# A hybrid decoder trunk: stream, embeddings and output transposed by the host, layer 0 projected before its norm

## The chip, the core and the metric

The kernel runs on one core of a Trainium2 chip. The metric is the device time of one launch in microseconds (us); what the host does before and after the launch is not in it. Most runs of one kernel agree within 0.3%.

## The reference

A sequence of 2048 tokens of width 1024 in float32 passes two layers. Layer 0 is half retention, half stick-breaking attention (4 heads of 128 each), layer 1 is an RWKV-7 recurrence (16 heads of 64). Each layer is followed by a gated embedding p, and the stream ends in an RMS norm.

```python
def rmsnorm(x, gain):
    y = xf * lax.rsqrt(jnp.mean(xf * xf, axis=-1, keepdims=True) + RMS_EPS)
    return y * gain
for i in range(2):
    hn = rmsnorm(h, norm_gain[i])
    if i % 2 == 0:   # z = hn @ w_in, split in q, k, v, gate of both groups
        h = h + even_mixer(hn, even_w_in, even_w_out, ret_gn_gain)
    else:
        h = h + rwkv7_mixer(hn, ...)
    gate = sigmoid(h @ ple_gate[i])
    h = h + gate * (p[i] @ ple_proj[i])
return rmsnorm(h, final_gain)
```

The factor 1/rms of a token is one number per row of hn, so `(x * gain / rms) @ w` equals `(x * gain) @ w` with each row scaled by 1/rms afterwards.

## The kernel before

The tokens go through in two halves of 1024 (`w` = 0, 1), in blocks of 512 (`TB`) or tiles of 128. Operands of the large projections are exact splits of float32 into two parts, hi and lo (`split`, L215 and L216), and each product is three matmuls (`mm3`, L246 to L248). `proj_T` gives results with a channel on a partition, `proj_N` with a token on a partition.

The order of the work: half 0 of layer 0 (`l0_norm`, `retention`, `stick`, `tail`), half 0 of layer 1's projections (`l1_proj`), half 1 of layer 0 (`l0_norm_next`, `retention`, `stick`), then layer 1's recurrence of half 0 merged with half 1's tail (`tail_lean`), `l1_proj` of half 1, the recurrence of half 1 merged with a further `tail_lean`, and a last `tail` over 512 tokens with the rest of the final norm beside it. A generator per piece says in what order instructions are written; a planner then places them on each engine by its own costs. Each engine and each DMA queue (SP's, ScalarE's, POOL's) works through its list in order.

What the change touches:

- `load_vectors` (L177) gathers nine vectors by DMA, and TensorE transposes them.
- `l0_norm` (L323): x comes in rows (a token on a partition). ScalarE sums squares (L342), VectorE forms 1/rms (`rsqrt`), two matmul groups spread it over partitions (L348), TensorE transposes x (L377), one copy goes to DRAM as the residual `xT` (L380), VectorE multiplies by gain and 1/rms (L382), and the result is split.
- `next_stats` (L386) does squares and transposes (L407) for half 1, beside half 0's tail (`SIDE` = 2 steps per block of channels), and writes x transposed and 1/rms to DRAM; `l0_norm_next` (L427) loads and multiplies them (L439).
- In `retention`, `tok` (L485) evacuates a projection: q and k scaled by a table's column (L488, L489), v copied, the gate through Silu (L492). In `stick`, the evacuations (L571 and L584) make hi on ScalarE and lo on VectorE from PSUM and write both to DRAM; a gate is copied by ScalarE.
- `tail` and `tail_lean` load p in rows and transpose it (L774, L950). The last `tail` transposes the stream (L831), and after 1/rms eight products on ScalarE and VectorE (L844, L846) precede the writes (L848). `finish` (L851) loads the kept stream in pieces of 128 floats, transposes (L868), scales on ScalarE (L870) and writes rows of the output.

Of the kernel before, what the change touches and what calls it, by code (L numbers as in the profile page):

```python
# [9 lines left out]
F32 = mybir.dt.float32  # L10
F32R = mybir.dt.float32r
BF16 = mybir.dt.bfloat16
# [10 lines left out]
HT = 1024  # tokens of one pass over the layers  # L23
# [4 lines left out]
RH = 4  # retention heads  # L28
SH = 4  # stick-breaking heads
NH = 16  # rwkv heads  # L30
C = 64  # rwkv chunk
# [27 lines left out]
# columns of the table of constants  # L59
# [14 lines left out]
# per-channel vectors, one row block of 8 x 128 each  # L74
# [30 lines left out]
def interleave(*gens):  # L105
    """Emit several generators in turn; each is (generator, steps per turn)."""
# [11 lines left out]
def merge(a, b, ratio, tc=None, ahead=0):  # L118
    """Emit two generators so that the costs they yield grow in step, those of b counted `ratio` times."""
# [14 lines left out]
class Trunk:  # L134
    def __init__(self, ctx, tc, ins, out):
# [19 lines left out]
        # states that pass from one half of the tokens to the next  # L155
# [3 lines left out]
        self.rs_kept = self.cst.tile([P, NHALF * NTT], F32, name="rs_kept")  # L159
        self.dd = {}  # L160
# [16 lines left out]
    def load_vectors(self):  # L177
        nc, i = self.nc, self.i
        flat = lambda a: a.rearrange("(b p) -> b p", p=P)
        rows = [  # L180
            (V_G0, i["norm_gain"].rearrange("j (b p) -> (j b) p", p=P)),
            (V_GF, flat(i["final_gain"])),
            (V_W0, flat(i["rwkv_w0"][0])),
            (V_A0, flat(i["rwkv_a0"][0])),
            (V_KK, flat(i["rwkv_k_k"][0])),
            (V_KA, flat(i["rwkv_k_a"][0])),
            (V_RK, i["rwkv_r_k"][0].rearrange("(b h) n -> b (h n)", h=2)),
            (V_MU, i["odd_mu"][0].rearrange("j (b p) -> (j b) p", p=P)),
            (V_GN, flat(i["ret_gn_gain"][0])),
        ]  # L190
        n = V_N * NB
        v = self.cst.tile([P, n], F32, name="vec")
        with self.tc.tile_pool(name="vl", bufs=1) as vl, self.tc.tile_pool(name="vps", bufs=1, space=PSUM) as vps:
            t = vl.tile([n, P], F32, name="vrows")
            nc.gpsimd.memset(t, 0.0)
            for j, src in rows:
                nc.sync.dma_start(t[j * NB : j * NB + src.shape[0], :], src)
            yield
            ps = vps.tile([P, n], F32, name="vt")
            nc.tensor.transpose(ps, t, self.ident[:n, :n])  # L200
            nc.vector.tensor_copy(v, ps)
        self.vec = v
        # 1 - mu and 1 - k_a
# [14 lines left out]
    def weights(self, src, shape):  # L218
        """src: list of (AP of the raw tile's part, AP in DRAM)"""
# [30 lines left out]
    def proj_T(self, w, acts, evac, psp, ts=range(NTB), t0=0):  # L250
        """out[channel, token] of one block of channels, blocks ts of tokens; those of acts begin with block t0"""
# [30 lines left out]
    def proj_N(self, ws, acts, evac, psp):  # L282
        """out[token, 512 columns], the token tiles two by two"""
# [39 lines left out]
    def l0_norm(self, w):  # L323
# [3 lines left out]
        with (  # L327
# [31 lines left out]
            for t in range(4):  # L359
                load(t)  # L360
# [1477 lines left out]
```

## Time and profile before

| | |
|---|---|
| median of 3 runs | 3897.31 us (3895.5 to 3903.19) |
| profiled execution: span | 3894.4 us (no other time of it is given) |
| TensorE busy | 3605.5 us, 93% |
| VectorE busy | 2249.9 us, 58% |
| POOL busy | 1882.7 us, 48% |
| ScalarE busy | 1540.2 us, 40% |
| granted TensorE clock, mean | 0.935 |
| moved by DMA | 488.01 MB, 125 GB/s |

The span runs from the first to the last instruction. Busy times come from the hardware profiler; matmuls overlap, so the sum of their durations is more than the time that they take. The granted clock is a share of 2.4 GHz.

### The profile page before, as it was taken

To read this page: it belongs to the slowest core of one execution; us is meant where nothing else is said; L and a number is where in the kernel's file an instruction comes from. 1 tells how busy PE (TensorE), PEld (TensorE's weight loads), DVE (VectorE), ACT (ScalarE), POOL (GpSimd) and SP (SyncE) were. 2 spreads that over 40 slices of the span, in tenths; PEclk is the share of its full clock that TensorE was granted. 3 is DMA by queue.
4 is the path that set the end of the run, shared out by engine and by line. 5 is a ranking of instruction groups with operands and counts; after the bars stand their busy time and mean duration, and the time that the engine had idled before them with its cause. 6 is when DMAs were issued, how large, how long until landed. Compare 5 with 4: busy or idle time off the path is not lost. (4 is left out here: it accounts for less than half of the span.)

```text
span 3894.4 us, 67082 instructions
## 1 busy us (share of the span) xinstructions
PE 3605.5 (93%) x25961; PEld 2822.9 (72%) x25961; DVE 2249.9 (58%) x3876; ACT 1540.2 (40%) x2892; POOL 1882.7 (48%) x1590
## 2 busy tenths in 40 slices
PE   8999999899998999998989999799988899999978
PEld 6888878677665788887767777577656677777757
DVE  4434442455777433557866756654777577667442
ACT  4223443345433332545533333355343243333344
POOL 4345544554565444655534435454564244434455
PEclk9999999899999999999989989699999899968889
DMA  4126554322455213436355534322446554444273
GB/s 158 33 82 191 151 169 138 109 95 71 138 155 178 70 55 116 141 101 139 83 150 146 149 104 122 85 84 81 142 143 204 142 147 136 119 114 128 84 234 122
DMA packets 670982, 488.01 MB, mean 125 GB/s; under 512 B 180436, under 2 KB 554056, under 8 KB 670664
## 3 DMA queue, kind: packets, MB, share of 16 engines
q1 hardware_dynamic: 587240, 390.77, 34.8%
q10 hardware_dynamic: 42848, 59.39, 4.2%
q0 software_dynamic: 40576, 33.56, 3.8%
q8 instruction: 205, 3.36, 0.4%
q14 instruction: 113, 0.93, 0.1%
HBM read 333.51 MB, written 150.08 MB: 124 GB/s over the span
## 5 line engine op out<-in xcount | busy, mean ns | idle before, releaser
L216 POOL TENSOR_TENSOR wlo<-wraw,whi 128x1024 fp32r<-128x1024 f32 (+1 forms) x262 | 617.3, 2360 | 538.1 <-ACT whi L215 492.9
L246 PE MATMUL pj<-act,whi 128*128 128x512 f32 x1216 | 499.1, 414 | 23.8 <-ACT act L215 15.3
L247 PE MATMUL pj<-act,whi 128*128 128x512 f32 x1216 | 501.2, 412 | 6.5 <-DVE act L216 5.7
L248 PE MATMUL pj<-act,wlo 128*128 128x512 f32 x1216 | 498.1, 411 | 4.5 <-POOL wlo L216 4.5
L215 ACT CAST whi<-wraw 128x1024 fp32r<-128x1024 f32 (+1 forms) x262 | 263.9, 1010 | 328.6 <-PE pj L247 143.7
L247 PE MATMUL pj<-xs,whi 128*128 128x512 f32 x768 | 316.2, 412 | 17.1 <-POOL xs L216 10.2
L246 PE MATMUL pj<-xs,whi 128*128 128x512 f32 x768 | 305.1, 415 | 28.9 <-ACT xs L215 27.7
L248 PE MATMUL pj<-xs,wlo 128*128 128x512 f32 x768 | 310.3, 405 | 0.0
L246 PEld LDWEIGHTS pj<-act,whi 128*128 128x128 f32 x1216 | 238.7, 197 | 76.7 <-ACT act L215 17.4
L247 PEld LDWEIGHTS pj<-act,whi 128*128 128x128 f32 x1216 | 238.6, 196 | 62.6 <-DVE act L216 11.3
L248 PEld LDWEIGHTS pj<-act,wlo 128*128 128x128 f32 x1216 | 238.9, 196 | 56.4 <-POOL wlo L216 5.9
L216 POOL TENSOR_TENSOR xs<-mxa,xs 128x512 fp32r<-128x512 f32 x138 | 206.5, 1512 | 143.1 <-ACT xs L215 141.1
L246 PE MATMUL pj<-whi,act 128*128 128x512 f32 x640 | 258.9, 409 | 8.8 <-ACT whi L215 4.4
L247 PE MATMUL pj<-wlo,act 128*128 128x512 f32 x640 | 256.5, 401 | 1.8 <-POOL wlo L216 1.7
L248 PE MATMUL pj<-whi,act 128*128 128x512 f32 x640 | 255.3, 401 | 0.0
L669 DVE TENSOR_TENSOR_SCAN rr<-om,rr,ones 128x512 f32<-128x512 f32 (+3 forms) x160 | 219.4, 1376 | 55.2 <-ACT om L663 42.7
L678 POOL TENSOR_TENSOR be<-be,rr 128x512 f32<-128x512 f32 (+3 forms) x160 | 168.1, 1052 | 158.7 <-DVE rr L669 85.2
L1125 DVE SCALAR_TENSOR_TENSOR mxa<-hn,vec,mxa 128x512 f32<-128x512 f32 x192 | 193.5, 1027 | 57.5 <-ACT mxa L1123 55.3
L246 PEld LDWEIGHTS pj<-xs,whi 128*128 128x128 f32 x768 | 148.2, 196 | 90.1 <-ACT xs L215 42.3
L247 PEld LDWEIGHTS pj<-xs,whi 128*128 128x128 f32 x768 | 149.8, 195 | 73.1 <-POOL xs L216 23.3
L248 PEld LDWEIGHTS pj<-xs,wlo 128*128 128x128 f32 x768 | 150.0, 195 | 37.3 <-issue 6.2
L1437 PE MATMUL g<-xr,kb 64*128 64x128 f32 x1024 | 147.0, 308 | 25.1 <-DMA xr<-ar 11.8
(355 smaller groups left out, 8388.4 us busy)
## 6 DMA issues: line engine op xcount, KB each, us to landing
wraw<-in_odd_w_in SPq DMA_DIRECT2D x64, 512.0 KB, 4.5
kb<-kb SPq DMA_DIRECT2D x64, 512.0 KB, 3.0
wraw<-in_ple_gate SPq DMA_DIRECT2D x56, 512.0 KB, 4.7
wraw<-in_even_w_in SPq DMA_DIRECT2D x64, 256.0 KB, 3.2
wraw<-in_even_w_in SPq DMA_DIRECT2D x32, 512.0 KB, 3.8
ar<-ar SPq DMA_DIRECT2D x32, 512.0 KB, 2.7
w<-v SPq DMA_DIRECT2D x128, 128.0 KB, 3.4
xr<-ar SPq DMA_DIRECT2D x64, 256.0 KB, 5.1
```

The costliest lines, as they stand in the source:

```text
L215: nc.scalar.copy(hi, src)
L216: (lo_eng or nc.vector).tensor_tensor(lo, src, hi.bitcast(F32), op=ALU.subtract)
L246: nc.tensor.matmul(ps, a[0], b[0], start=first, stop=False)
L247: nc.tensor.matmul(ps, a[0], b[1], start=False, stop=False)
L248: nc.tensor.matmul(ps, a[1], b[0], start=False, stop=last)
L669: nc.vector.tensor_tensor_scan(rr[:, 0:kw][:, ::-1], om[:, ::-1], self.ones.to_broadcast([P, kw]), rr[:, kw : kw + 1], op0=ALU.mult, op1=A ...
L678: nc.gpsimd.tensor_tensor(be, be, rr[:, 1 : kw + 1], op=ALU.mult)
L1125: nc.vector.scalar_tensor_tensor(a, hn[d][:, sl], self.col(V_MU + p, d), a, op0=ALU.mult, op1=ALU.add)
L1437: nc.tensor.matmul(ps[:, j], kb[br, 4 * g + j], xr[br, par, 4 * g + j], start=True, stop=True)
```

## The change

The host passes x also transposed (`xT`, channels by tokens), p transposed (`pT`) and the per-channel vectors as one table (`vec`); the output is written as channels by tokens and the host transposes it. `l0_in` takes the place of `l0_norm`, `next_stats` and `l0_norm_next` in both halves. Comments and docstrings go too.

```diff
+    def l0_in(self, w):
+        self.xT = [self.i["xT"][d * P : (d + 1) * P, tokens] for d in range(NB)]
+            for tb in range(NTB):
+                for d in range(NB):
+                    x = sb.tile([P, TB], F32, tag="x", bufs=8)
+                    nc.sync.dma_start(x, self.xT[d][:, sl])
+                    nc.scalar.activation(hi, x, AF.Copy, scale=g)
+                    nc.vector.scalar_tensor_tensor(lo, x, g, hi, op0=ALU.mult, op1=ALU.subtract)
+                    if d % 2:
+                        t = tb * 4 + d // 2
+                        xt = sb.tile([P, D], F32, tag="xt")     # bufs=2
+                        nc.scalar.dma_start(xt, self.i["x"][0, r0 : r0 + P, :])
+                        nc.scalar.activation(sq, xt, AF.Square, accum_out=st[:, t : t + 1])
+            for tb in range(NTB):
+                rs = self.rsqrt(sb, st[:, ts], 1.0 / D, RMS_EPS, 4, "rs")
+                nc.vector.tensor_copy(self.rs0[:, ts], rs)
+                ... four matmuls spread rs over partitions (rbp), as L348
+                nc.scalar.copy(rb, rbp)
+                nc.sync.dma_start(self.rb0[:, tb * TB : (tb + 1) * TB], rb)
 # retention: qks = rs0 times the table's columns
-                    nc.scalar.activation(qk[:, 0], ps[:, 0:128], AF.Copy, scale=self.k[:, C_QS + h : ...])
-                    nc.vector.tensor_copy(v, ps[:, 256:384])
-                    nc.scalar.activation(sg[:, t], ps[:, 384:512], AF.Silu)
+                    nc.scalar.activation(qk[:, 0], ps[:, 0:128], AF.Copy, scale=qks[:, t, h : h + 1])
+                    nc.vector.tensor_scalar_mul(v, ps[:, 256:384], rs)
+                    nc.scalar.activation(sg[:, t], ps[:, 384:512], AF.Silu, scale=rs)
 # stick: v's split with the scale rs0 (same count); q, k, g:
+                        f = sb.tile([P, TB], F32, tag="pf", bufs=1)
+                        nc.vector.tensor_tensor(f, ps, rbs[t], op=ALU.mult)
+                        if nm == "g":
+                            nc.scalar.dma_start(dst[0, :, sl], f)
+                            return
...
-                            self.split(ps, hi, lo)
+                            self.split(f, hi, lo)
 # tail and tail_lean: p without transposes
-                        nc.tensor.transpose(tps[d][:, j], pr[:, d * P : (d + 1) * P], self.ident)
+                    nc.sync.dma_start(pr, i["pT"][l, d * P : (d + 1) * P, t0_ : t0_ + TB])
+                    self.split(pr, pT[d][0][:, tok(q)], pT[d][1][:, tok(q)])
 # the last tail, after 1/rms; finish does the same with x loaded from h
+                rbp = self.rows_of(rs[:, ...], pt)      # four matmuls
+                for ob in range(NB):
+                    nc.vector.tensor_tensor(o, rbp, h1[ob][:, tok(t)], op=ALU.mult)
+                    (nc.scalar if ob % 2 else nc.sync).dma_start(self.out_at(w, ob, t), o)
```

## Rows read from the trace of the kernel before

**Rows 1.** Page, first part: busy us, share of the span, instructions of each engine.

```profile
PE 3605.5 (93%) x25961; PEld 2822.9 (72%) x25961; DVE 2249.9 (58%) x3876; ACT 1540.2 (40%) x2892; POOL 1882.7 (48%) x1590
```

**Rows 2.** Windows of 60 us: each engine's busy us (instructions), clock, DMA share, GB/s.

```profile
0.00:60.00 60.00, 41.12 (x187) 32.79 (x188) 32.60 (x59) 38.24 (x70) 26.96 (x25) 0.97 0.65 220
...
420.00:480.00 60.00, 60.00 (x347) 52.35 (x346) 31.49 (x36) 27.91 (x62) 34.12 (x47) 1.00 0.52 143
...
600.00:660.00 60.00, 60.00 (x289) 49.35 (x288) 15.62 (x31) 21.77 (x41) 21.40 (x16) 1.00 0.41 124
...
3720.00:3780.00 60.00, 38.10 (x175) 29.80 (x174) 30.56 (x52) 27.45 (x42) 29.12 (x18) 0.77 0.85 263
```

**Rows 3.** TensorE by line: xcount | busy us, mean ns | idle before.

```profile
L868 PE MATMUL ft<-k,fx 128*128 128x128 f32 x96 | 14.7, 292 | 2.6 <-ACT fo L870 2.4 <-DMA fx<-h 0.2
...
L377 PE MATMUL xp<-k,x 128*128 128x128 f32 x64 | 12.9, 341 | 12.0 <-DMA x<-in_x 7.0 <-DVE hf L382 3.5 <-DVE rs L318 1.6
...
L407 PE MATMUL nt<-k,nx 128*128 128x128 f32 x64 | 9.4, 272 | 0.0
...
L950 PE MATMUL pt<-k,pr 128*128 128x128 f32 x40 | 7.6, 321 | 8.1 <-DMA pr<-in_p 7.4 <-DVE pT L216 0.7
...
L831 PE MATMUL ft<-k,h 128*128 128x128 f32 x32 | 4.7, 276 | 2.4 <-ACT h L816 1.9 <-ACT fo L833 0.5
...
L774 PE MATMUL pt<-k,pr 128*128 128x128 f32 x24 | 4.2, 276 | 0.2
L348 PE MATMUL rbp<-k,rs 128*128 128x128 f32 x16 | 3.2, 364 | 5.6 <-DVE rs L319 5.6
L421 PE MATMUL nr<-k,ns 128*128 128x128 f32 x16 | 2.1, 275 | 0.0
```

**Rows 4.** Timeline of TensorE, first tail: start us, us, operation, count.

```profile
562.64 0.39 PE L246 MATMUL pj<-act,whi 128*128 128x512 f32 x1
562.87 0.60 PE L407 MATMUL nt<-k,nx 128*128 128x128 f32 x4
563.22 0.49 PE L247 MATMUL pj<-act,whi 128*128 128x512 f32 x1
563.54 0.39 PE L248 MATMUL pj<-act,wlo 128*128 128x512 f32 x1
```

**Rows 5.** Timelines of POOL and of ScalarE, first norm.

```profile
24.39 4.68 POOL L216 TENSOR_TENSOR wlo<-wraw,whi 128x1024 fp32r<-128x1024 f32 x2 [1.45 <-DMA wraw<-in_even_w_in]
...
50.09 0.37 ACT L488 ACTIVATE qk<-pj,k 128x128 f32<-128x128 f32 x1
```

**Rows 6.** Windows, instructions on pj alone, first 60 us.

```profile
0.00:60.00 60.00, 28.65 (x102) 20.24 (x103) 0.57 (x2) 3.02 (x10) 0.97 0.65 220
```

**Rows 7.** Timeline of TensorE at the second half's start.

```profile
1290.27 0.50 PE L246 MATMUL pj<-whi,act 128*128 128x512 f32 x1 [2.28 <-ACT sg L492]
```

**Rows 8.** Instructions on tile x, count: ns min/median/max, first, last start.

```profile
L342 ACT ACTIVATE sq<-x x8: 1056/1057/1058, 5.1 to 17.9; 128x1024 bf16<-128x1024 f32 x8
...
L216 DVE TENSOR_TENSOR act<-x,act x8: 677/1268/1786, 1259.5 to 1285.9; 128x512 fp32r<-128x512 f32 x8
```

**Rows 9.** Waits of TensorE: us in total, times, longest.

```profile
PE pt L950 <- DMA pr<-in_p: 7.4, 2, 5.8
```

**Rows 10.** Timeline of the end, all engines.

```profile
3879.87 0.69 DVE L812 TENSOR_TENSOR ssacc<-ssacc,g 128x512 f32<-128x512 f32 x1 [0.76 <-ACT g L810]
...
3881.93 1.66 PE L1029 MATMUL ssp<-ones,ssacc 128*128 128x1 f32 x8
...
3886.52 4.03 SPq L848 DMA_DIRECT2D out<-fo  x8
```

**Rows 11.** Groups of VectorE, 300 to 545 us.

```profile
L593 DVE SCALAR_TENSOR_TENSOR pst<-pj,pst 128x512 fp32r<-128x512 f32 x6 | 4.1, 688 | 5.7 <-ACT pst L592 5.7
```

**Rows 12.** DMA issues: count, KB each, median us to landing.

```profile
dg<-pst ACTq DMA_DIRECT2D x16, 256.0 KB, 2.0
```

**Rows 13.** Waits of TensorE, 300 to 545 us.

```profile
PE ot L247 <- DVE wT L216: 0.9, 1, 0.9
```

More of the change, by code (lines that the diff above doesn't have):

```diff
@@ L177, in load_vectors @@
     def load_vectors(self):
[L178 to L201, printed above, removed]
+        nc = self.nc
+        v = self.cst.tile([P, V_N * NB], F32, name="vec")
+        nc.scalar.dma_start(v, self.i["vec"])
         self.vec = v
@@ L564, in stick @@
             sb = pool("sk", 2, side="right")
+            rbs = []
+            for t in range(NTB):
+                rbs.append(sb.tile([P, TB], F32, tag=f"rb{t}", name=self.u("rb"), bufs=1))
+                nc.sync.dma_start(rbs[t], self.rb0[:, t * TB : (t + 1) * TB])
             def vproj():
@@ L824, in tail @@
                     next(side, None)
-                if l and ob % 4 == 3:
-                    ft.append([])
-                    for k, t in enumerate(tts):
-                        tp = pt.tile([P, 4, P], F32, tag="pt", name=self.u("ft"))
-                        for j in range(4):
-                            nc.tensor.transpose(tp[:, j], h1[ob - 3 + j][:, t * P - t0 : (t + 1) * P - t0], self.ident)
-                        o = sb.tile([P, TB], F32, tag="fo", name=self.u("fo"), bufs=8)
-                        (nc.vector.tensor_copy if k % 2 else nc.scalar.copy)(o, tp.rearrange("p a b -> p (a b)"))
-                        ft[-1].append(o)
             for _ in side:
@@ L839, in tail @@
             rs = self.token_rstd(sb, pt, tts=tts)
-            for q in range(2):
-                for n, t in enumerate(tts):
-                    o = ft[q][n]
-                    if (q + n) % 2:
-                        nc.scalar.activation(o, o, AF.Copy, scale=rs[:, n : n + 1])
-                    else:
-                        nc.vector.tensor_scalar_mul(o, o, rs[:, n : n + 1])
-                    r0 = w * HT + t * P
-                    nc.sync.dma_start(self.out[0, r0 : r0 + P, q * TB : (q + 1) * TB], o)
@@ L852, in finish, with rows_of, load @@
+    def rows_of(self, rs, pool):
+        rbp = pool.tile([P, TB], F32, tag="pt", name=self.u("rbp"))
+        for j in range(4):
+            self.nc.tensor.matmul(
+                rbp[:, j * P : (j + 1) * P], rs[:, j : j + 1].to_broadcast([P, P]), self.ident, start=True, stop=True
+            )
+        return rbp
+    def finish(self, w, h, rs, ts, sb, pt):
         nc = self.nc
-        def load(t, q):
-            x = sb.tile([P, 4, P], F32, tag="fx", name=self.u("fx"), bufs=3)
-            nc.sync.dma_start(x, h[:, 4 * q : 4 * q + 4, t * P : (t + 1) * P])
+        def load(t, ob):
+            x = sb.tile([P, TB], F32, tag="fx", name=self.u("fx"), bufs=3)
+            nc.sync.dma_start(x, h[:, ob, t * TB : (t + 1) * TB])
@@ L947, in block @@
                 if ob < 2:
-                    tp = pp.tile([P, 4, P], F32, tag="pp", name=self.u("pt"))
-                    for j in range(4):
-                        nc.tensor.transpose(tp[:, j], pr[:, j], self.ident)
                     x = tuple(sb.tile([P, TB], F32R, tag=f"pT{ob}{j}", name=self.u("pT")) for j in range(2))
-                    self.split(tp.rearrange("p a b -> p (a b)"), x[0], x[1])
+                    self.split(pr, x[0], x[1])
                     pT.append(x)
@@ L1757, in side @@
             def side(sb, pt):
-                yield from self.finish(w - 1, h2[0], self.rs_kept, range(NTT), sb, pt)
-                yield from self.finish(w, h2[1], self.rs_kept[:, NTT:], range(4), sb, pt)
+                yield from self.finish(w - 1, h2[0], self.rs_kept, range(NTB), sb, pt)
+                yield from self.finish(w, h2[1], self.rs_kept[:, NTT:], range(1), sb, pt)
             self.tail(1, w, mB, gB, h1, side, [1])
@@ L1827 @@
     given = {n: inputs[n] for n in _INS}
+    given["xT"] = np.asarray(inputs["x"])[0].T
+    given["pT"] = np.asarray(inputs["p"])[:, 0].transpose(0, 2, 1)
+    given["vec"] = vectors(inputs)
     given["c_mat"], given["c_rope"], given["c_eye"] = constants()
@@ L1832 @@
         ins[name] = nc.dram_tensor(f"in_{name}", a.shape, mybir.dt.from_np(a.dtype), kind="ExternalInput").ap()
[L1833 removed]
+    out = nc.dram_tensor("out_0", (D, S), F32, kind="ExternalOutput").ap()
     with tile.TileContext(nc, schedule_with_timeline_sim=True) as tc:
```

201 lines of the change are left out of this document (71 added, 130 removed).

## The prediction

> **What bounds the kernel now.** I read the page's busy shares first: TensorE is busy in 93% of the span, the next engine in 58% [rows 1]. A share is a mean over stages, so the table of windows comes next. It shows three kinds of stretch [rows 2]: in attention and in the first tail (420 to 480, 600 to 660) TensorE is busy for all 60.00 us at granted clock 1.00 (2.4 GHz), so there each instruction taken off TensorE gives its slot back; in the first 60 us it is busy for 41.12 us, transposes among them; and where the last tail begins (3720 to 3780) for 38.10 us, with DMA at 0.85, so there it waits for something else. Then the groups of TensorE's instructions, where the transposes that go stand as lines of their own [rows 3], then the timeline, for what one of them costs.
>
> The sum is made against the profiled execution: 3894.4 us of span. The page gives no other time for that execution; the median of the runs, 3897.3, lies 2.9 us (0.07%) above it, and I add that at the end.
>
> **What one transpose costs.** A group's mean (272 ns) is no price, since matmuls overlap. In the timeline a 512-column matmul starts 0.23 us after the one before it; with four transposes between, 0.90 us pass from 562.64 to 563.54, in which two such matmuls and the four also start [rows 4]. 0.90 less two slots of 0.23 leaves 0.44 us for four: 0.11 us each. Removed are 64 (xp), 64 (nt), 96 (ft in the finish), 32 (ft of the last tail), 40 and 24 (p) [rows 3], 320 in all, or 35 us of slots. New are four row broadcasts (4 matmuls, which the profile shows as 8 instructions), against two that go with the nt group; the two of the first norm stay and come again in the second half: 48 instructions more and 16 less, about 4 us at 0.11 where they fall into a full stretch; they are counted stage by stage.
>
> **Stage by stage.**
>
> *First norm, 0 to 60 us.* Before, the first projection matmul needs loaded x, sums of squares, 1/rms, its broadcast, transposes, a product, and a split. The first evacuation starts at 50.09 [rows 5]. In the 60 us the projection gets 102 matmuls in [rows 6], 23.5 us of work at 0.23. After, x arrives transposed; a ScalarE copy scaled by the gain and a VectorE difference make the operands, and 1/rms is first needed at the evacuation. What is late then: the first pair of token tiles needs 8 tiles of x (2 MB), 4 chunks of weights (2 MB) and, for its scale, 4 tiles of x with a token on a partition (2 MB); at the 220 GB/s of this window [rows 2] that is 29 us, and POOL's lo parts of the weights take 2.34 us each (4.68 for two [rows 5]), 9.4 for four. I put the end of the first pair at 26 to 33 us; the other 54 of the 102 matmuls take 12.4 more, so the same work is done at 38 to 45: 15 to 22 earlier. Taken: -16. Other end: ScalarE works in order, and each sum of squares waits for a 512 KB load behind which the next copy stands; if they and their loads all stood in the path, nothing would be gained (0). Upper end -24.
>
> *First tail, 540 to 725.* The side work for the next half goes: 64 transposes (7.0 us) and 16 broadcast instructions (1.8); of the p transposes 16 (1.8). TensorE is full here, so all count: -10.6. The scaled copies and writes that go with them only free ScalarE and its DMA queue. Nothing is late next, since the tail's own matmuls follow back to back.
>
> *Second half's norm, from 1256.* Its x is loaded long ahead, as before. The chain is one step shorter and POOL does no lo parts, but ScalarE gets eight squares of 128x1024, with eight loads of 512 KB on its queue. Before, TensorE here waits 2.28 us for an evacuation behind a busy ScalarE [rows 7]. The squares need only x, so they can run during the stage before. -3, between +8 (eight squares of 1.057 [rows 8] in the path) and -6 (that wait and the POOL parts).
>
> *Tails beside the recurrence.* 40 transposes, 4.4 us, of which I count 4. Two waits of TensorE for the load of p cost 7.4 us [rows 9]; the wait then falls on ScalarE's split, which nobody needs until the embedding's product. But the recurrence's matmuls behind it soon wait for other engines, so -3 of 7.4. Sum -7 (0 to -12).
>
> *Last tail.* 96 transposes, but about 30 lie where TensorE waits anyway (3720 to 3780 [rows 2]); 66 are 7.3 us, the broadcasts cost 2.3: -5. Eight p transposes -0.9, the first 16 of the 32 ft -1.8. The finish's product moves from ScalarE to VectorE, 24 of 0.69, and VectorE is half idle there; without that cover they would cost up to 17. Sum -7.
>
> *The end.* Before, the squares are added up by 3880.56 but their sums over partitions start at 3881.93, behind transposes and copies; after 1/rms two engines share eight products, and eight writes are issued from 3886.52 for 4.03 us, to 3890.55 [rows 10]. After: those 1.4 go; the broadcast adds 1.6 (half of L348's 3.2 [rows 3]), so the first write could go at 3888.2, and seven more products on one engine take 4.8 at 0.688 [rows 11], with two queues for the writes: the last at 3893.0, less the 1.4 at 3891.6. +1.1 (0 to +5).
>
> *Stick-breaking heads.* The projections are now unnormalised, so each of 48 evacuations gets a product with the 1/rms row into one buffer, f. Nearest row for a PSUM operand: 0.688 us [rows 11], 33 us of VectorE over two halves, in stretches where it is about half busy (31.49 of 60 [rows 2]). For q and k the second product waits until f is read; for g until f is written out, 2.0 us [rows 12]. Behind it on VectorE stand the attention's scans and splits, for which TensorE's transposes and products wait. The PSUM bank, on the other hand, is free after one operation instead of two. The bounds: -2 (banks free earlier) and +77 (33, plus 8 x 2.0, plus 16 x 1.8, all reaching TensorE). I take +4, near the low end, because TensorE's wait for these splits was 0.9 us in the whole first attention [rows 13].
>
> Here a rule weighs against the change. The rows show that a lo part read from PSUM takes 0.688 us [rows 11], and that one whose two inputs are in SBUF takes 0.677 at least but 1.268 in the median, in a stretch with POOL at work beside it [rows 8]. The Trainium skill (SBUF — State Buffer, on the engine-side ports) says that a VectorE instruction with two SBUF inputs and a GpSimd instruction that reads SBUF take one shared port pair in turn, whole instructions at a time. The 32 lo parts of q and k move from PSUM to f, so by the rule they become the slow kind. By the rows of PSUM reads alone they cost nothing new; by the other row 32 x 0.58, or 19 us of VectorE, and POOL is held as long. With the rule I would take +8 instead of +4 for this stage.
>
> **Sum.** -16 -10.6 -3 -7 -7 +1.1 +4 = -38.5. 3894.4 - 38.5 = 3855.9, plus 2.9: **3859 us**. Its own range is 3838 to 3882.
>
> **Rivals.**
> 1. *The work was hidden anyway.* Only the full stretches give: the first tail (-10.6) and a third of the rest, with the start held by the loads of x in both layouts and of weights. -10.6, -3 for that third, +1.1 and +4 make -8.5: 3889. For it: DMA at 0.65 in the first window, 0.85 at the last tail [rows 2]. Against it: before, the first evacuation comes at 50.09, far behind the 29 us that the loads need.
> 2. *VectorE becomes the bound of the attention.* The product into the single buffer f, in order ahead of the scans, stalls TensorE in every evacuation: +77 instead of +4, so 3932. It decides once more than about half of these stalls (38 of 77) reach TensorE; above that the kernel is slower than before. Against it: VectorE at about half and a bank that is freed sooner.
> 3. *More than the slots comes back.* The start gives 24, the p waits all 7.4, the second norm 6, and the low-clock stretches behind these waits (0.77 in 3720 to 3780 [rows 2]) rise: 3835.
>
> Chances: forecast 0.62, rival 1 0.16, rival 2 0.11, rival 3 0.11. About 0.2% (8 us) is what a measurement of this kernel can tell from no change. Faster: forecast, rival 3 and half of rival 1, 0.81; no change, 0.07, and 0.01 of slower are the rest of rival 1; with rival 2, slower is 0.12. The range for 8 of 10 goes from 3830, short of rival 3's far side, to 3898, past rival 1.
>
> **What would show it.** Right: no ft, nt, xp or pt transposes; first evacuation between 26 and 36 us; the first tail's matmuls 10 us shorter; in the attention TensorE at 59 or more of 60 us and waits on wT and rr under 5 us in each half. Wrong: first evacuation after 42 us; TensorE idle before ot or tp behind VectorE's f; a gap over 5 us at the second half's start with ScalarE waiting for xt; or a last write more than 6 us after the last 1/rms step's former distance of 4.6 us.

## The result: slower by half a per cent

The changed kernel takes 3920.8 us (median of 18 runs, 3900.7 to 3935.3), the kernel before 3898.2 in the same session (18 runs, 3876.2 to 3912.7): a ratio of 1.0056, 95% interval 1.0040 to 1.0072, 22.6 us more where I had forecast 38 less. The profiled execution of the changed kernel is one of its quicker ones (3909.1 us, span 3907.3), so the profiles, 3894.4 against 3907.3, show 12.9 of these 22.6 us. What follows says where the 12.9 lie.

The page, first part, of the changed kernel:

```profile
PE 3565.7 (91%) x25672; PEld 2797.0 (72%) x25672; DVE 2285.1 (58%) x3951; ACT 1504.8 (39%) x2796; POOL 1859.2 (48%) x1573
```

TensorE has 289 instructions and 39.8 us of work less than in [rows 1], and the span is still longer: it stands idle more. The groups of TensorE by line show that the transposes are gone and what came for them (the groups of [rows 3] other than L348 have no counterpart; L336 is L348, now in both halves):

```profile
L767 PE MATMUL rbp<-k,rs_kept 128*128 128x128 f32 x24 | 5.5, 428 | 1.2 <-ACT y L1514 1.2
L336 PE MATMUL rbp<-k,rs 128*128 128x128 f32 x32 | 5.2, 317 | 4.0 <-ACT ev L1074 2.9 <-DVE rs L299 1.1
L767 PE MATMUL rbp<-k,rs 128*128 128x128 f32 x8 | 2.1, 441 | 2.4 <-DVE rs L299 2.4
```

The windows of [rows 2], changed kernel:

```profile
0.00:60.00 60.00, 31.85 (x139) 25.65 (x140) 25.21 (x54) 31.58 (x55) 16.90 (x17) 1.00 0.73 238
420.00:480.00 60.00, 59.21 (x338) 51.00 (x337) 37.15 (x42) 26.93 (x60) 31.96 (x47) 1.00 0.53 143
600.00:660.00 60.00, 60.00 (x266) 49.72 (x265) 13.78 (x20) 17.99 (x29) 27.25 (x20) 1.00 0.23 72
3720.00:3780.00 60.00, 27.32 (x247) 21.80 (x246) 35.71 (x73) 16.36 (x24) 28.31 (x19) 0.71 0.72 213
```

In the attention VectorE has 5.7 us more to do in 60 and TensorE is no longer quite full; in the first tail TensorE is full as before, without the side work. To see where time goes, the span is cut at four places that both traces have (first load of the first tail's input, m<-mx; first sum over partitions behind it, ssp; last copy of an attention's output, mo<-ot; last write of y by the second recurrence, yT<-yo):

```
stretch                                       before    after     difference  forecast
layer 0 of the first half                      506.0    508.1       +2.1       -16, +2
first tail                                     228.4    212.7      -15.7       -10.6
projections, layer 0 of the second half       1226.2   1231.4       +5.2       -3, +2
both tails beside a recurrence, projections   1786.7   1821.2      +34.5       -7
last tail to the end                           147.1    133.9      -13.2       -7, +1.1
```

The +4 of the stick-breaking heads is split evenly over the halves here.
The two tails gave more than forecast, 28.9 us. The first half of layer 0 gave nothing. And the long fourth stretch, whose code hardly changed, took back 34.5. That stretch alone, by windows from the last mo<-ot to the last yT<-yo (us, busy us of PE, PEld, DVE, ACT and POOL with instructions, clock, DMA share, GB/s); first the kernel before:

```profile
1960.60:3747.30 1786.70, 1636.46 (x15640) 1238.64 (x15638) 1163.61 (x2132) 664.57 (x1180) 817.23 (x554) 0.90 0.46 129
```

and the changed one:

```profile
1952.20:3773.40 1821.20, 1629.63 (x15304) 1238.81 (x15304) 1167.63 (x2133) 659.34 (x1170) 816.60 (x553) 0.88 0.47 128
```

TensorE's idle time there is the length of the stretch (1786.70) less its busy time (1636.46): 150.2 us before, 191.6 after. With 336 instructions fewer it is busy nearly as long, at a granted clock of 0.88 in place of 0.90 of 2.4 GHz. This idle time is the number by which most experiments below are read. It is not the whole of the time: total time is also the place where the stretch begins, and TensorE's busy time in it.

The same stretch in three parts, up to the last y of the first recurrence, from there to the first y of the second, and the second recurrence; first the kernel before:

```profile
1960.60:2520.60 560.00, 508.61 (x6156) 394.24 (x6154) 363.91 (x798) 197.78 (x370) 250.41 (x165) 0.88 0.48 128
2520.60:3147.50 626.90, 574.97 (x3004) 415.28 (x3003) 411.65 (x505) 261.60 (x426) 304.33 (x215) 0.94 0.46 136
3147.50:3747.30 599.80, 552.88 (x6484) 429.11 (x6482) 388.05 (x830) 205.18 (x385) 262.48 (x175) 0.88 0.45 122
```

and the changed one:

```profile
1952.20:2517.30 565.10, 504.21 (x5846) 391.25 (x5847) 362.71 (x776) 193.90 (x361) 247.31 (x162) 0.85 0.48 125
2517.30:3161.20 643.90, 578.75 (x3020) 421.31 (x3020) 407.75 (x508) 261.48 (x427) 308.14 (x217) 0.93 0.45 133
3161.20:3773.40 612.20, 546.66 (x6446) 426.25 (x6442) 397.17 (x850) 203.97 (x383) 261.15 (x175) 0.86 0.48 126
```

The idle time grows in all three, by 9.5, 13.2 and 18.6 us, and the time by 5.1, 17.0 and 12.4: most of the loss lies behind the end of the first recurrence.

### The profile page after: what moved, and what is told of

Read it like the earlier page. It is cut to its first block, busy times and chain, and to the rows that moved or that the text cites. A ratio compares the mean times of both kernels' runs of the same rounds, so it can differ in the third digit from the quotient of the medians.

```text
span 3907.3 us, 66284 instructions
## 1 busy us (share of the span) xinstructions
PE 3565.7 (91%) x25672; PEld 2797.0 (72%) x25672; DVE 2285.1 (58%) x3951; ACT 1504.8 (39%) x2796; POOL 1859.2 (48%) x1573
## 5 line engine op out<-in xcount | busy, mean ns | idle before, releaser
L1350 PE MATMUL g<-xr,kb 64*128 64x128 f32 x1024 | 143.0, 314 | 37.7 <-DMA xr<-ar 21.2
```

Source lines behind the costliest of these rows:

```text
L1350: nc.tensor.matmul(ps[:, j], kb[br, 4 * g + j], xr[br, par, 4 * g + j], start=True, stop=True)
```

## The experiments

Each has a median over its own runs, as a ratio to the kernel before on the same chip, and one profile of one execution. All in one table (A: start of the last mo<-ot; idle: TensorE's idle time from A to the last yT<-yo; last y: that write, in the profile's us):

```
label        ratio   95% interval       A       idle   last y
(before)     1                          1960.6  150    3747
b_null1      0.9982  0.9967 to 0.9996   1958.8  158    3757
b_null2      1.0045  1.0028 to 1.0063   1965.4  163    3787
b_leanpT     1.0045  1.0029 to 1.0060   1955.7  169    3759
b_out        0.9993  0.9976 to 1.0010   1958.2  172    3767
(after)      1.0056  1.0040 to 1.0072   1952.2  192    3773
a_null1      1.0067  1.0043 to 1.0090   1947.2  192    3785
a_null2      1.0073  1.0050 to 1.0096   1953.1  191    3794
a_r093       1.0032  1.0016 to 1.0048   1947.4  185    3769
a_r097       1.0044  1.0026 to 1.0062   1955.3  189    3776
a_start      1.0026  1.0010 to 1.0042   1948.6  186    3777
a_inplace    1.0087  1.0064 to 1.0109   1942.2  185    3789
a_both093    1.0093  1.0065 to 1.0120   1931.4  193    3786
k_95_93      1.0057  1.0038 to 1.0076   1930.2  202    3775
leanp_back   1.0074  1.0051 to 1.0096   1950.7  197    3788
leanp_r093   1.0016  1.0001 to 1.0031   1946.2  184    3760
a_pstage     1.0083  1.0068 to 1.0098   1950.4  193    3791
l_98_93      1.0007  0.9993 to 1.0021   1937.3  184    3766
s_95_93      0.9987  0.9973 to 1.0001   1939.1  187    3763
b_l0         1.0087  1.0064 to 1.0111   1949.7  199    3799
```

**Is it p beside the recurrence, or chance?** In the last recurrence of the changed kernel the waits of TensorE have a row that the kernel before doesn't have, in place of [rows 9]:

```profile
PE pp L226 <- ACT pw L195: 8.4, 1, 8.4
...
PE yt L1546 <- DVE y L1541: 21.6, 3, 11.1
```

The new row is the first, the product pp. The wait for y was there before, and shorter:

```profile
PE yt L1633 <- DVE y L1628: 9.2, 3, 6.0
```

The transposes of p had shared one PSUM bank with the embedding's product pp. My first theory was that without them the planner puts that product early. The rival: the planner writes a new order for everything behind any edit, and that alone costs time. Four kernels, two of them with null edits:

```diff
 leanp_back, on the changed kernel: p beside a recurrence as before
-                    pr = T("g", 2)
+                    pr = early.tile([P, 4, P], F32, tag="g", ...)      # and i["p"], four transposes into pp, split
 b_leanpT, on the kernel before: the same lines the other way round
 a_null2 on the changed kernel, b_null2 on the kernel before
-RATIO_B = 0.95
+RATIO_B = 0.96
```

> The changed kernel, with one part undone: the tail that runs beside a recurrence loads p with a token on a partition again and transposes it on TensorE (40 transposes in five blocks). The changed kernel measured 3921 us against 3898 before. Theory A (the embedding's product): with the transposes gone from the one bank that they shared with that product, the product is ordered early on TensorE and waits there for its weights, with the recurrence behind it; in the last recurrence the profile shows 30 us lost. Then undoing this part gives most of that back less about 4 us of transposes: 3893 to 3903, and TensorE's wait of 8.4 us for pw in the last recurrence is gone. Theory B (written order by chance): the planner sorts both recurrences anew after any edit near them, and that alone moves the time by 10 to 30 us; then this kernel lies anywhere from 3895 to 3935 and the order differs from both kernels. Theory C (the loss is in the start, the attention and the projections): no change, 3917 to 3927.

> The kernel before, with this one part of the change alone: the tail beside a recurrence loads p transposed by the host and splits it from SBUF; 40 transposes go. Theory A: the loss comes with this part, 3915 to 3930 (17 to 32 us over before). Theory B: the recurrences are sorted anew, and the time lies anywhere from 3885 to 3920, without a growing wait for pw to explain it. Theory C: my prediction's own term, 4 to 7 us faster, 3890 to 3895.

> The changed kernel with a null edit: the ratio in which the last recurrence and the tail beside it are emitted goes from 0.95 to 0.96. The same instructions, in another written order, from the last recurrence on alone. Theory B: the last recurrence's time differs from the changed kernel's by 8 us or more, up or down. Theories A and C: within 6 us of the changed kernel, 3915 to 3927, since each instruction's work and each wait's cause are the same.

> The kernel before with the same null edit (ratio 0.95 to 0.96). Theory B: the total differs from before by 8 us or more, up or down, most likely up, since 0.95 was chosen with this kernel's own order: 3906 to 3925. Theories A and C: within 6 us of before.

Measured: 1.0074, 1.0045, 1.0073 and 1.0045. Undoing this part on the changed kernel gives nothing back; its wait goes and another comes in its place, for the load of p:

```profile
PE pt L869 <- DMA pr<-in_p: 10.0, 2, 9.7
```

Theory A fails. The null edit costs the kernel before 0.45%, as much as b_leanpT does, so that b_leanpT's loss (19 us, as much as theory A asked for) can't be told from a change of order. Theory B holds for the kernel before; the null edit of the changed kernel moved it by 5.6 us (3926.4 against 3920.8), less than the 8 that B asked for. How wide does the order scatter? Same edit, other values:

```diff
-RATIO_B = 0.95
+RATIO_B = 0.9501      # a_null1, b_null1; a_r093: 0.93; a_r097: 0.97
```

> The changed kernel, ratio of the last recurrence 0.95 to 0.9501: a smaller null edit; the written order differs from the middle of the last recurrence on alone. So far null edits cost the kernel before 18 us and the changed one 5. Theory B1 (the order of the kernel before is a lucky one; any other is worse by about 18 us, for either kernel alike): the last recurrence takes 770 to 790 us as in the changed kernel, the total lies at 3912 to 3930. Theory B2 (the orders of the changed kernel scatter as widely, and good ones exist for it too): one of this run and the two with 0.93 and 0.97 is at 3900 or below.

> The changed kernel, ratio 0.95 to 0.93 (the tail is emitted a little later beside the recurrence). B1: 3912 to 3930. B2: at 3900 or below in one of the three orders. Both expect the first 2000 us as in the changed kernel to within 3 us.

> The changed kernel, ratio 0.95 to 0.97. B1: 3912 to 3930. B2: at 3900 or below in one of the three orders.

> The kernel before, ratio 0.95 to 0.9501; the order differs from the second half of the last recurrence on alone. B1: slower by 8 to 20 us, 3902 to 3915. A kernel whose time doesn't hang on the order: within 5 us of before.

B1 falls: another order of the kernel before is as good (0.9982). B2 falls too: no order of the changed kernel came to 3900. Orders differ by some 10 us either way (3889 to 3912 for the kernel before, 3906 to 3926 for the changed one), but their means, 3900 and 3917, lie 17 us apart (medians of the session's runs, three and five orders). So chance in the order is a part of the 22.6 us and, as far as three and five orders can tell, not the larger one. The fourth stretch of the table of stretches scatters in the same way: 1787, 1798 and 1822 us in the three orders of the kernel before, 1820 to 1841 in the five of the changed one, so that its 34.5 is 26 between the means. The idle column parts the two sorts more sharply: 150 to 163 against 185 to 192. But it doesn't give the time by itself: in b_null2, slower by 0.45%, 22 of the 35 us that the stretch is longer are TensorE's busy time (1821.7 less 163.1, against 1636.5), with nearly the same number of instructions.

**The start and the buffer f.** These are read in their own stages, in front of the recurrences. Note that a_start carries two edits, the order of the loads and the place of the squares.

```diff
 a_start: weights of the first retention head ahead of x; squares behind the copies of a block
+            if w == 0:
+                self.first = self.ret_load(0)      # the loads of load(0), moved here from retention
...
-                    if d % 2:
-                        t = tb * 4 + d // 2        # xt, its load, its square
+                for t in range(tb * 4, tb * 4 + 4):
+                    ...
 a_inplace: no buffer f
-                        f = sb.tile([P, TB], F32, tag="pf", name=self.u("pf"), bufs=1)
+                        f = st[:, 1].bitcast(F32)  # lo is formed in place
```

> The changed kernel, with two edits in the first norm: the weights of the first retention head are loaded ahead of x, and the sums of squares come behind the eight copies of a block of tokens. In the changed kernel TensorE's first projection matmul waits until 26.65 us for weights that stand behind x in both layouts, and the first evacuation is at 48.08 us (50.09 before), where I had forecast 26 to 33. Theory S (order of the loads: the third and fourth chunk of weights come late because the first two come late): the first evacuation at 30 to 38 us, and the first tail's first load at 494 to 500 us in place of 508.1. Rival S2 (the DMA has to bring 6 MB or more anyway): the first evacuation after 44 us, the tail's load within 3 us of 508. The total also carries a new order of the recurrences, plus or minus 10.

> The changed kernel, without the single buffer f: the product with 1/rms is written where the lo part goes, and the lo part is formed in place, so that two evacuations can be under way. My rival 2 in its small form (f's single buffer holds up VectorE in the attention): the attention of the first half ends 2 to 4 us earlier (first tail's first load at 504 to 506 in place of 508.1), the stretch from the end of the first tail to the end of the last attention (1231 us, 1226 before) 5 to 9 us shorter. Otherwise (the product's own 0.69 us on VectorE is what costs, or the start): both within 2 us.

Timelines of TensorE and of ScalarE at the start, changed kernel (start us, us, operation, count, idle before it and who ended it):

```profile
26.65 2.08 PE L226 MATMUL pj<-whi,act 128*128 128x512 f32 x4 [26.65 <-ACT whi L195]
...
23.90 0.72 ACT L321 ACTIVATE act<-x,vec 128x512 fp32r<-128x512 f32 x1 [6.77 <-DMA wraw<-in_even_w_in]
...
25.56 1.03 ACT L195 CAST whi<-wraw 128x1024 fp32r<-128x1024 f32 x1
...
48.08 0.37 ACT L404 ACTIVATE qk<-pj,qks 128x128 f32<-128x128 f32 x1 [4.30 <-PE pj L228]
```

and a_start:

```profile
13.82 0.79 PE L226 MATMUL pj<-whi,act 128*128 128x512 f32 x1 [13.82 <-ACT act L323]
...
37.09 0.37 ACT L406 ACTIVATE qk<-pj,qks 128x128 f32<-128x128 f32 x1 [1.49 <-PE pj L228]
```

The first evacuation comes 11.0 us earlier and the first tail's input 9.4 (498.7 against 508.1): theory S holds, and S2 falls. The moved squares were not run apart, but in the changed kernel ScalarE's idle time ahead of its first cast of weights ends with the load of wraw at 23.90, and only one copy and one square stand between (to 25.56), so the loads' order is what held the first matmul. Before, POOL formed two lo parts of weights from 24.39 to 29.07 us [rows 5]; in the changed kernel the weights are no earlier (ScalarE's first cast of them is at 25.56), since they are loaded behind nine tiles of x. The raw weights have two buffers, so chunks three and four follow only when the first two are split.

Without f the first tail's input comes 5.1 us earlier (503.0), a little more than the 2 to 4 that were expected. In the second half the stretch to the last attention is 1224.3 us here and 1222.9 to 1231.8 in the four other kernels without f, against 1226.8 to 1236.6 in those of the table with f: some 4 us in the mean, inside the scatter. That it was the waiting and not the product shows in VectorE's groups, 300 to 545 us of the changed kernel (what answers to [rows 11]):

```profile
L512 DVE TENSOR_TENSOR pf<-pj,rb 128x512 f32<-128x512 f32 x20 | 13.5, 673 | 8.4 <-PE pj L228 6.1 <-DMA dg<-pf 2.2
L522 DVE SCALAR_TENSOR_TENSOR pst<-pf,pst 128x512 fp32r<-128x512 f32 x6 | 9.8, 1635 | 3.1 <-ACT pst L521 3.1
L196 DVE TENSOR_TENSOR pst<-pf,pst 128x512 fp32r<-128x512 f32 x6 | 8.3, 1378 | 3.8 <-ACT pst L195 3.8
```

and of a_inplace:

```profile
L522 DVE SCALAR_TENSOR_TENSOR pst<-pst 128x512 fp32r<-128x512 f32 x6 | 9.8, 1631 | 1.4 <-ACT pst L521 1.4
L196 DVE TENSOR_TENSOR pst<-pst 128x512 fp32r<-128x512 f32 x6 | 8.5, 1462 | 1.1 <-ACT pst L195 1.1
```

The product costs 0.673 us as forecast. A lo part took 0.688 from PSUM [rows 11] and takes 1.38 to 1.64 in the mean from f. It stays as slow without f; the waits ahead of it shrink, from 3.1 and 3.8 us to 1.4 and 1.1. The means hide two kinds. Timeline of POOL and VectorE, changed kernel:

```profile
408.05 2.39 POOL L196 TENSOR_TENSOR wlo<-wraw,whi 128x1024 fp32r<-128x1024 f32 x1 [2.82 <-ACT whi L195]
...
408.54 2.45 DVE L522 SCALAR_TENSOR_TENSOR pst<-pf,pst 128x512 fp32r<-128x512 f32 x1 [1.37 <-ACT pst L521]
...
448.80 0.68 DVE L196 TENSOR_TENSOR pst<-pf,pst 128x512 fp32r<-128x512 f32 x1
```

Where POOL forms a lo part of weights (2.39 us, from SBUF) as the instruction starts, it ends some 0.55 us after POOL's; with no POOL instruction beside it, it takes 0.68 to 0.69, as from PSUM.

But the totals of both kernels don't follow: a_inplace is with b_l0 the second slowest of all. Both edits together, and p on TensorE with another ratio:

> Both edits (weights ahead of x, no buffer f) with the ratio 0.93, which gave 3906 in the changed kernel. If the stages add and the order is as good as with 0.93: 3906 less 8 to 14 for the start less 5 to 10 for the attention, 3882 to 3893, that is below the kernel before (3895). If the recurrences' order is drawn anew with each edit: anywhere from 3880 to 3915, with the gain up to the end of the last attention (13 to 24 us) still there.

> The changed kernel with the p of the tail beside a recurrence transposed on TensorE again, ratio 0.93. The last recurrence and the last tail together took 914 to 937 us in five orders of the changed kernel, 909 in the one order with this part undone, 896 to 911 in three orders of the kernel before. Theory A in a smaller form (this part costs some 10 us there in the mean over orders): 900 to 912 us again. Theory B (order alone): as often above 914 as below.

In a_both093 the attention ends at 1931.4, 20.8 us ahead of the changed kernel and 29.2 ahead of the one before: the stages add, within the 13 to 24 us expected. The last y is then written at 3786, later than in either, and the time, 3932, is above both ranges that were given. leanp_r093 took 898.6 us for the last recurrence and last tail, about as theory A in its small form has it, and a total of 1.0016. Down the whole table A goes from 1930 to 1955 in the fifteen kernels with the new layer 0 and the last y doesn't follow it (A 1930.2, last y 3775; A 1955.3, last y 3776).

**Two more ideas.** Last recurrence and last tail together are counted from the first copy bs<-bnp of that recurrence to the end of the span. With the new layer 0 the last recurrence alone (first to last yT<-yo) took 608 and 594 us where p was transposed on TensorE, 612 to 636 in the eight kernels where the host's p lay in the buffers g, which the next block's gates need. And four kernels, in whose order the tail's matmuls end early beside the first recurrence, were some 18 us longer from the attention to the end of the second projections. Two theories, one for each, and kernels that combine their cures:

```diff
 a_pstage, on the changed kernel: p in two of the eight buffers of the staged inputs
-                    pr = T("g", 2)
+                prs.append(T("stage", NB))         # ahead of the loop over ob
 l_98_93: a_start, a_inplace, leanp_back, RATIO = 0.98, RATIO_B = 0.93
 k_95_93: a_start, a_inplace, RATIO = 0.95, RATIO_B = 0.93
 s_95_93: a_start, a_inplace, a_pstage, RATIO = 0.95, RATIO_B = 0.93
```

> The changed kernel, with one edit: beside a recurrence p is loaded into two of the eight buffers of the staged inputs, ahead of the output projection, and no longer into the two buffers g, which the gates of the next block and the sigmoids need too and which it holds until ScalarE and VectorE have split it. Theory G (the held buffer costs the 20 us): last recurrence and last tail together 895 to 912 us (changed kernel: 913 to 937 in eight orders). Theory T (the product in the bank that the transposes shared goes early): 913 to 937 still. By the order's count (63 of the tail's matmuls left beside the end of the first recurrence, as in the slow kind) the first merged stretch with the projections behind it should take some 1059 us, which costs the total 18.

> The changed kernel with weights ahead of x, without f, with p transposed on TensorE beside a recurrence, ratios 0.98 and 0.93. In its written order 264 matmuls of the tail stand beside the last eight transposition groups of the first recurrence (161 to 266 in the nine kernels that took some 1041 us there, 88 to 117 in the four that took 1059). If that count decides: 493.6 + 212 + 1225 + 1041 + 904 = 3876 of span, 3875 to 3888 as the median, 10 to 25 below the kernel before. If it doesn't: 1059 there and 3893 to 3906.

> The same without the transposes (p from the host in the buffers g, as in the changed kernel), ratios 0.95 and 0.93; 234 of the tail's matmuls beside the end of the first recurrence, though the last of them stands 112 instructions ahead of its end, as in the slow kind. If the count decides: 1041 in that stretch; if the place of the last one decides: 1059. The last two stages as in the changed kernel, 913 to 937: total 3885 to 3910 or 3903 to 3928.

> Weights ahead of x, no f, p from the host in the staged inputs' buffers, ratios 0.95 and 0.93 (233 of the tail's matmuls beside the end, the last 56 ahead of it). Theory G and the count: 493.6 + 212 + 1225 + 1041 + 905 = 3877 of span, a median of 3875 to 3888. Theory T: 3890 to 3912.

Last recurrence with last tail: 911.9 in a_pstage, 891.9 and 899.3 in l_98_93 and s_95_93, 934.8 in k_95_93, near what theory G says in all four, though 911.9 lies at the edge of both theories. The total doesn't follow: what goes there comes back beside the first recurrence, whose last y comes 576 to 593 us after A in the five kernels with the cure (p on TensorE or in the staged inputs' buffers), against 555 to 570 in the others of the table with the new layer 0, but for a_inplace, a_both093 and b_l0 (581 or 582 each). From there to the first y of the second recurrence the two sorts don't differ: 633 to 647 us with the cure, 642 to 650 without (b_l0: 653). b_l0 below, with p on TensorE too, took 615 for the last recurrence. The count of matmuls fails too: it promised 1059 us for a_pstage (1063 measured), but 1041 for the other three (1073, 1050, 1067). The totals of l_98_93 (3903) and s_95_93 (3899) lie outside the ranges that went with the cures (3875 to 3888). Why the one recurrence loses what the other gains was not tried. The best of these, s_95_93, is as fast as the kernel before, with the 21.5 us by which its attention ends earlier used up.

**Which part brings the idle time?** The change cut in two; with b_leanpT above, three:

```diff
 b_l0: l0_in, retention, stick, x and p of the first and last tail from the host as changed; rest as before
 b_out: finish, the end of the last tail and the output's layout as changed; rest as before
```

> The kernel before with the first part of the change alone: layer 0 projects the unnormalised stream, x comes from the host transposed (and p of the first and last tail, which stand outside the recurrences). Output pass, and p beside the recurrences, as before. Theory L (this part brings the idle time, through what it does to the order and the queues where the last attention passes into the first recurrence): TensorE idle 184 to 202 us between the end of the last attention and the last write of y, total 3912 to 3930. Theory O (the output part does): idle 150 to 169, the gain up to the last attention stays: 3882 to 3895.

> The kernel before with the last part of the change alone: the final norm is a product with a broadcast of 1/rms and the output is written transposed. Theory L: idle 150 to 169 us in that stretch, the last tail 9 us shorter, 3884 to 3900. Theory O: idle 184 to 202, 3910 to 3925.

The stretch A to last y, of b_l0:

```profile
1949.70:3798.70 1849.00, 1650.46 (x15352) 1253.75 (x15352) 1175.61 (x2124) 663.51 (x1176) 808.05 (x553) 0.87 0.46 125
```

and of b_out:

```profile
1958.20:3767.00 1808.80, 1636.64 (x15630) 1240.20 (x15628) 1174.54 (x2140) 660.39 (x1174) 817.87 (x554) 0.89 0.45 127
```

198.5 us idle against 172.2; in time, 1.0087 against 0.9993. Theory L comes nearer in both, but not all of it came: b_out's 172.2 and its time (3900.7) lie just above the ranges given for it, b_l0's time (3936.9) above its own, and b_out's last tail is 4 us shorter, not 9. Both profiles are of the slowest execution of their kernel, so that both idle times may be high. So layer 0's part brings most of the idle time; a small share of the other two parts is not excluded (169 and 172 against 150 to 163). Over all profiles the five kernels with the old layer 0 have 150 to 172 us, the fifteen with the new one 184 to 202, whatever else was varied. The added idle time has no one place. Summed over all waits of TensorE in the stretch, those that VectorE ended are 78 us in the mean of the fifteen and 63 in that of the five, those that ScalarE ended 68 and 58, those that a DMA ended 21 and 24.

## Why the prediction was wrong

*First norm, -16: wrong.* I added up the bytes that the first pair of tiles needs (29 us at 220 GB/s) and left out in which order the queue brings them. The weights stand behind x, the first matmul waits until 26.65 us, and the first evacuation comes at 48.08 instead of 50.09, past the 42 that I had named as a sign of being wrong. Counted as the forecast counts, the 102nd projection matmul starts at 59.8 us before, at 56.1 in the changed kernel and at 42.3 in a_start, inside the 38 to 45 that I had named. Windows with the instructions on pj alone, as in [rows 6], of the kernel before, the changed one and a_start:

```profile
0.00:59.80 59.80, 28.45 (x102) 20.04 (x102) 0.57 (x2) 3.02 (x10) 0.97 0.65 221
0.00:56.10 56.10, 26.20 (x102) 20.08 (x103) 0.69 (x2) 3.25 (x10) 1.00 0.77 253
0.00:42.40 42.40, 26.54 (x102) 20.77 (x103) 0.69 (x2) 2.90 (x10) 1.00 0.92 305
```

(The first evacuation of a_start, 37.09, is later than the 26 to 33 because 84 projection matmuls, not 48, are placed ahead of it.) The start's size was right, with the loads in the other order. Of the 13.8 us between the changed kernel and a_start there, 9.4 are left at the first tail.

*First tail, -10.6: right in mechanism, small in size* (-15.7; in the other orders of both kernels the same to within 2 us). The slots came back, with 5 us more than at 0.11 us each; what these 5 are was not tried.

*Stick-breaking heads, +4 for both halves: too small.* 5.1 us go with f in the first half alone, and some 4, inside the scatter, in the second; what the product costs beyond that was not run apart. TensorE's waits in the first attention stay under 5 us (3.3 us, for wT at tp and z). Rival 2 as a large loss did not come; that the measured 3920.8 lies near its 3932 is chance. In this trace a lo part with both inputs in SBUF takes 2.45 us when it starts within POOL's 2.39, and 0.68 alone. This agrees with the Trainium skill (SBUF — State Buffer, section "SBUF: two separate sides"), which says that a VectorE instruction with two SBUF inputs and a GpSimd instruction that reads SBUF hold the shared port pair in turn, each for the whole instruction. Over the whole kernel the 32 lo parts of q and k took 44.3 us of VectorE in place of 21.6 (the two groups' busy times), near the 19 us that I had worked out for the rule, but TensorE felt little of it: a_inplace keeps the slow form and still gains.

*Second half's norm, -3:* not to be separated; the whole stretch lost 5.2. The wait for sg of [rows 7] is gone, and no wait of TensorE from 1200 to 1310 us is longer than 2.9 us (3.4 before), so the gap that I had named as a sign of being wrong didn't come.

*Last tail and end, -5.9: not contradicted, but the measured -13.2 is partly chance.* The last stretch takes 147.1, 142.7 and 137.2 us in the three orders of the kernel before and 131 to 138 in the five of the changed one, 8 us less between the means; b_out, which has this part alone, takes 143.0. (My own terms for the last tail add up to -7.7, and I entered -7.) From the last sum of squares to the last write it took 11.7 us, 10.0 before [rows 10], +1.7 for the +1.1 forecast. The end of the changed kernel:

```profile
3891.59 0.69 DVE L735 TENSOR_TENSOR ssacc<-ssacc,g 128x512 f32<-128x512 f32 x1 [0.76 <-ACT g L733]
...
3896.64 2.07 PE L767 MATMUL rbp<-k,rs 128*128 128x128 f32 x8 [2.44 <-DVE rs L299]
3898.75 4.88 DVE L757 TENSOR_TENSOR fo<-rbp,h 128x512 f32<-128x512 f32 x8 [2.17 <-PE rbp L767]
3899.47 3.92 SPq L758 DMA_DIRECT2D out<-fo  x4
3900.07 3.92 ACTq L758 DMA_DIRECT2D out<-fo  x4
```

*Tails beside the recurrence, -7: this step failed, and it decided the sign.* The stretch took 34.5 us more, so 41.5 of the 51.4 us between forecast and profile lie here, and 16 in the first half of layer 0; the other stages gave 6 back. I took the order of the work there as given and priced 40 transposes and two waits in it. The order was not given, and TensorE's idle time in it, for which I had no term, grew from 150.2 to 191.6 us. The planner orders both recurrences anew, and with the new layer 0 it puts more of the first recurrence ahead of the last attention's end: by the windows from 0 to A, TensorE has 9921 instructions there in the changed kernel and 9773 in the one before, although 160 transposes and broadcasts went and 16 came, so 292 were moved in. In the kernels without f and with p from the host it is 9761 (a_inplace, a_both093, k_95_93, s_95_93), so 132 moved in, and their idle time is no less. The first recurrence's writes of y, kernel before:

```profile
L1638 SPq DMA_DIRECT2D yT<-yo x64: 520/608/1766, 1945.7 to 2520.6; - x64
```

and the changed one:

```profile
L1551 SPq DMA_DIRECT2D yT<-yo x64: 519/608/1860, 1917.9 to 2517.3; - x64
```

They begin 27.8 us earlier and end 3.3 us earlier: of the 8.4 us by which the attention ends earlier, 5.1 are gone by the end of the first recurrence. From there on the changed kernel loses 29.4 more, 17.0 up to the second recurrence's first y and 12.4 beside it. One of the places is in SP's queue where attention passes into recurrence. Changed kernel:

```profile
1949.49 2.36 SPq L1322 DMA_DIRECT2D xr<-ar  x2
1952.02 2.41 SPq L1333 DMA_DIRECT2D w<-v  x4
...
1962.17 0.62 SPq L1324 DMA_DIRECT2D kb<-kb  x1
1962.83 0.66 SPq L634 DMA_DIRECT2D mx<-mo  x1
1966.94 2.23 SPq L822 DMA_DIRECT2D stage<-mx  x5
```

and before:

```profile
1960.99 0.34 SPq L707 DMA_DIRECT2D mx<-mo  x1
1962.84 1.76 SPq L903 DMA_DIRECT2D stage<-mx  x4
```

The last output of the attention, ready at 1952.2, is written at 1962.83, behind the recurrence's own loads and writes, and the tail that is to fill TensorE beside the recurrence gets its first input 14.7 us after the attention's end; in all five kernels with the old layer 0 it is 2.2. That is 12.5 us later, but up to the end of the first recurrence only 9.5 of the 41.4 us of added idle time lie. In a_inplace and a_both093 the same load comes 4 us after the end, and the idle time up to there is 68 and 65 us (61 in the changed kernel, 51 before), so this load is not shown to be a cause. Shown is that layer 0's part brings most of the idle time, that neither p, nor the output, nor one unlucky order does so alone, and that an earlier end of the attention is not passed on. How layer 0's part does it, through which decisions of the planner or otherwise, stays open; whether the lower granted clock in the stretch follows from the idle time or adds to the loss was not tried either.

Rival 1 had the right reason for the start (held by the loads), rival 2 the right buffer at about an eighth of its price (9 of 77 us, the second half's share inside the scatter), and none had the mechanism that decided.

## What to carry to other kernels

Where a planner writes the order, an edit changes the order of all that follows: measure a null edit first (here -0.2% and +0.45% for the same instructions), and read a change of about half a per cent by its stages and by the bottleneck engine's idle and busy time in each, over several orders, not by one total. For a start, list the loads in the order of their queue up to the first consumer, not only their bytes. And a gain in front of a long stretch counts only if that stretch's end moves: look for its last write before adding up what lies ahead of it.

## What was not expected of the hardware

Executions of one order differ more than the medians of several orders do: the changed kernel's 18 runs lie between 3901 and 3935 us, the medians of its five orders between 3906 and 3926. Up to the last recurrence TensorE's order is the same in the changed kernel and in a_null2; in 400 us beside the first recurrence the one gets through 4241 instructions and the other through 4426, at granted clocks of 0.88 and 0.91. The changed kernel:

```profile
1950.00:2350.00 400.00, 363.93 (x4241) 283.60 (x4240) 257.44 (x550) 136.56 (x257) 162.75 (x106) 0.88 0.54 138
```

and a_null2:

```profile
1950.00:2350.00 400.00, 367.09 (x4426) 288.10 (x4423) 266.36 (x565) 142.24 (x269) 167.54 (x111) 0.91 0.54 139
```

From A to the first recurrence's last y the five kernels that share this order (the changed one, a_null1, a_null2, a_r093, a_r097) took 555 to 567 us, one execution each. So one profile of such a stretch settles no 10 us. The idle column has one profile for each kernel; it rests on twenty of them together.
